# Hybrid attention and MLP block: every second output weight's low part on VectorE, the first weights in two transfers, two forced orders

## The chip, the cores and the metric

The kernel runs on one core of one Trainium2 chip. The metric is the device time of one execution in microseconds (us), as the median of several runs. The engines are named as in the profile: PE (TensorE), DVE (VectorE), ACT (ScalarE), POOL (GpSimd) and SP (SyncE, which issues the transfers of this kernel).

## The reference

One layer of a streaming encoder over x of 1 x 1024 x 1024, float32. Two groups of eight heads of 64 share one input projection: group A is sliding-window attention with two key/value heads and learned sinks, group B is attention over the own chunk of 64 and eight chunks before it, with a relative bias.

```python
n = rms_norm(h, norm1_g[layer])
proj = jnp.einsum('bsd,dp->bsp', n, w_in[layer])
qa, ka, va, qb, kb, vb = jnp.split(proj, split_at, axis=-1)
ya = mixer_a(...)            # sliding window, sinks
yb = mixer_b(...)            # softmax over a band of 9 chunks of 64 keys
y = jnp.concatenate([rms_norm(ya, out_norm_a_g[layer]),
                     rms_norm(yb, out_norm_b_g[layer])], axis=-1)
h = h + jnp.einsum('bsm,md->bsd', y, w_out[layer])
n2 = rms_norm(h, norm2_g[layer])
u = jnp.square(jax.nn.relu(jnp.einsum('bsd,df->bsf', n2, w_ff1[layer])))
h = h + jnp.einsum('bsf,fd->bsd', u, w_ff2[layer])
return rms_norm(h, final_norm_g)
```

## The kernel before

Every operand of a large product is kept as two parts: a high part, a rounded copy that ACT mostly writes, and a low part, the full value minus the high one. The low part is `split_l` (L170), a subtraction of two tiles on whichever engine its caller names; three products of parts stand for one product. So each operand costs one ACT copy and one subtraction on DVE or POOL, and PE's matmuls wait for both.

The program goes through the block in stages: the input projections (`ip_...`) and group A's attention, the transposes and projections of group B, group B's attention (`S_B` scores, `P_B` probabilities, `pt_B` transposes in PSUM, `T_B` their two parts, `av_B` the product with the values) with the output projection (`op_A`, `op_B`) between its pieces, and the MLP (`f`, `f_a`, `f_b`, `f_c`). PE's order is written out by hand and forced (`pe_order`); the other engines take their instructions in an order that a scheduler sets from the dependencies, and `after` (the dictionary is called `turned`) adds single forced orders: one instruction may not stand ahead of a marked one on its engine.

Head pairs of group B are numbered 0 to 7. `self.row` norms one row of probabilities by `rc_B` (L735, TENSOR_SCALAR, 128x640). `split_transposed` (L539) writes the high part of a transposed block T by ACT and the low one by DVE; `padL` is the last, half-empty block. PE's next `pt_B` and `av_B` wait for these.

The output weights w_out come in eight blocks `o0` to `o7` of 128 x 1024 (`out_weight`, L836). `load_weight` moves one block into a stage slot `st_o`, scales it by a gain in ACT for m = 2 and 3 (L221), writes the high part `w0_o` by ACT in two pieces of 128x512 (L222), and the low part `w1_o` by POOL in four pieces of 128x256. A stage slot is free again when the low part of the block in it is done, and a later block's transfer waits for that in SP's queue. o0 to o3 are made around 291 to 306 us, while PE works at the value projection `ip_vB` and group B's attention; o4 to o7 around 364 to 396 us, before `op_B`. Other work of POOL there is `h<-h,o` (L923), which adds the output `o` of `op_A` (L922, ACT) to the residual, and `sqB` (L624), sums of squares for the norm of group B.

At the start, SP moves the first block of x transposed and the first gains (`first`, L299), then the first weights (`first_w`, L300, 256 KB: k in its left half, q in its right), then `second` and others. DVE writes the high part `w_kA`, ACT that of q, and PE's first matmul `ip_kA` waits for them after some matmuls on zeros (`idle_ps`).

In the MLP, `operand` (L1054) splits the combined sums X of the activations, `combined` (L1082) and `sum_of` (L1111) make these sums; `prepare1` makes those for the weights ahead.

```python
return load_weight(w_out[m * P : (m + 1) * P, :], [P, D], f"o{m}", pool, 1, 2,
                   ogc[:, m : m + 1] if m in PLAIN else None)
```

Of the kernel before, what the change touches and what calls it, by code (L numbers as in the profile page):

```python
# [16 lines left out]
P = 128  # L17
SEQ = 1024
D = 1024
# [32 lines left out]
def kernel(  # L52
# [97 lines left out]

            return issue

    turned = {}

    def after(ins, mark=None, key=None):

        if mark:
            turned[mark] = ins.ins.name
        elif key in turned:
            dep = mybir.DependencyInfo(mybir.DependencyClass.NoSync, mybir.DependencyReason.DATA)  # L160
            tc.add_manual_dep(ins.ins, turned.pop(key), dep, reason="program order")

    def matmul(*args, **kw):
        pe(nc.tensor.matmul(*args, **kw))  # L164
# [4 lines left out]
    def split_l(engine, lo, full, hi):  # L169
        return engine.tensor_tensor(lo, full, f(hi), ALU.subtract)  # L170
# [102 lines left out]
    def load_start():  # L273

        ws = {kind: [page([P, NK, P], f"w{hl}_{name}") for hl in range(2)] for kind, _, name, _ in first_three}

        act, dve = InOrder(nc.scalar), InOrder(nc.vector)

        def split_w(kind, p, src, high, wait=False):
            hi, lo = (w[:, 2 * p : 2 * p + 2] for w in ws[kind])  # L280
            src = src.rearrange("p (a b) -> p a b", a=2)
            if high is dve:
                high.tensor_copy(hi, src)
            else:
                high.activation(hi, src, AF.Copy)

            def low():
                split_l(dve, lo, src, hi)

            return low if wait else low()  # L290

        def block(name):
            t = sp.tile([P, 2, HALF], F32, tag="xs", bufs=7, name=name)
            return t.rearrange("p a b -> p (a b)")


        b0, b1 = (block(f"x{k}") for k in range(2))
        w0 = sp.tile([P, D], F32, tag="xr", bufs=4, name="w0")
        nc.sync.dma_start(b0[:, : HALF + 8], first)  # L299
        nc.sync.dma_start(w0[:, :HALF], first_w)  # L300
        nc.sync.dma_start(b1[:, :HALF], second)
        nc.sync.dma_start(b1[:, HALF : HALF + 2 * P].rearrange("p (a b) -> p a b", a=2), w_in[VA0 // P][:, :2])
        dve.tensor_copy(g1c, b0[:, HALF : HALF + 8])
        low = split_w("k", 0, w0[:, : 2 * P], dve, True)
        split_xT(0, 0, b0[:, :HALF], b0[:, HALF : HALF + 1], act, dve)
        low()
        split_w("q", 0, w0[:, 2 * P : HALF], act)
        split_xT(0, 1, b1[:, :HALF], g1c[:, 1:2], act, dve)
        split_w("v", 0, b1[:, HALF : HALF + 2 * P], act)
        for k in range(2, NK):  # L310
            t = block(f"x{k}")
            n = HALF + 2 * P * len(WITH[k])
            nc.sync.dma_start(t[:, :n], start[k - 2][:, :n])
            split_xT(0, k, t[:, :HALF], g1c[:, k : k + 1], act, dve)
            for i, kind in enumerate(WITH[k]):
                c = HALF + 2 * P * i
                split_w(kind, k // 2, t[:, c : c + 2 * P], act)
        return [ws[kind] for kind in "kqv"]
# [217 lines left out]
        return [small.tile([P, 4], F32, tag=t, name=f"{t}_{name}") for t in ("nm", "sm", "rc")]  # L536

    def split_transposed(tp, T, lo, hi):
        after(nc.scalar.activation(T[:, 0, lo:hi], tp, AF.Copy), None, "ACT")  # L539
        low = split_l(nc.vector, T[:, 1, lo:hi], tp, T[:, 0, lo:hi])  # L540
        after(low, None, "DVE")
        turned["low"] = low.ins.name

    sq, late = {}, []

# [165 lines left out]
    class UnitB:  # L711
# [25 lines left out]
        def step(self, n):  # L737
            if n < len(self.kbs):
                self.turn(self.kbs[n])
            if n == 2 and late:  # L740
                turned["row"] = turned["low"]
                late.pop()()
            if n > 1:
                self.apply(self.kbs[n - 2])
# [88 lines left out]

    def out_weight(m):

        return load_weight(w_out[m * P : (m + 1) * P, :], [P, D], f"o{m}", pool, 1, 2, ogc[:, m : m + 1] if m in PLAIN else None)  # L836

    hres = {}

# [60 lines left out]
    def out_proj_a():  # L900
        ys, ws = [], []
        for m in range(4):
            ws.append(out_weight(m))
        for m in range(4):
            ys.append(load_y(m, (0,)))
        yield
        for tb in range(TB):
            if tb == 1:
                for m in range(4):
                    ys[m] += load_y(m, (1,))  # L910
            h = hres[tb] = page([P, D], f"h{tb}", F32)
            nc.sync.dma_start(h, x[tb * P : (tb + 1) * P, :])
            for dh in range(2):
                c = slice(dh * HALF, (dh + 1) * HALF)
                ps = aps.tile([P, HALF], F32, tag="w", bufs=3, name=f"op_A_{tb}_{dh}")
                for q in range(4):
                    out_proj_step(ps, ys, ws, q, tb, c)
                    if q == 3 and (tb, dh) == (TB - 1, 1):
                        yield
                    if q == 3:  # L920
                        o = main.tile([P, HALF], F32, tag="tst", bufs=2, name=f"o{tb}_{dh}")
                        nc.scalar.activation(o, ps, AF.Copy, scale=rA[:, tb : tb + 1])  # L922
                        nc.gpsimd.tensor_tensor(h[:, c], h[:, c], o, ALU.add)  # L923
                    if q < 3 or (tb, dh) != (TB - 1, 1):
                        yield
# [123 lines left out]
    def operand(p, n, g, src, engine):  # L1049

        if p not in X:
            X[p] = [[page([P, 2, HALF], f"X{p}{hl}{i}") for i in range(2)] for hl in range(2)]
        hi, lo = (X[p][hl][g][:, :, part(n)] for hl in range(2))
        nc.scalar.activation(hi, src, AF.Copy)  # L1054
        split_l(engine, lo, src, hi)

    def first_half(d, n, g):

# [49 lines left out]

    def sum_of(a, b, op, name, engine, alloc):
        t = alloc(name)  # L1110
        engine.tensor_tensor(t, a, b, op)  # L1111
        return t

    def second_operands(src, made, p, name, engine, alloc):
# [169 lines left out]
    for at, (n, p) in enumerate(order1):  # L1284
        if p == 3 and n > 0:
            load1(n + 1)
        ahead1 = at + (AHEAD1 + 1 if at < AT_ONCE else AHEAD1)

        behind = (n, p) == (0, 2)
        if ahead1 < len(order1) and not behind:  # L1290
            prepare1(*order1[ahead1], ahead1)
        product1(n, p)
        for work in chores.get((n, p), ()):
            combined(*work)
            if behind and work[0] == 5:
                prepare1(*order1[ahead1], ahead1)
        if n == NQ - 1:
            if p == 6:
                for i in range(LOAD2):
                    fetch2(i)  # L1300
            if p in (3, 7, 2):
                prepare2({3: 0, 7: 1, 2: 2}[p])
# [183 lines left out]
def _lay_out(inputs):  # L1486
    import numpy as np

    a = {n: np.ascontiguousarray(v) for n, v in inputs.items()}
    rel = a["rel_bias_b"][0]  # L1490
    far = np.repeat(rel[:, 256:], 512, axis=1)
    ext = np.concatenate([far, rel[:, 255:0:-1]], axis=1)
    band = np.stack([ext[:, 127 - p : 127 - p + 640] for p in range(128)], axis=1)
    d = -np.abs(128 + np.arange(128)[:, None] - np.arange(256)[None, :]).astype(np.float32)
    d[:64, 192:] = NEG
    d[64:, :64] = NEG
    og = np.concatenate([a["out_norm_a_g"][0], a["out_norm_b_g"][0]]).reshape(8, 128).T
    xT = a["x"][0].T.reshape(8, 128, 2, 512).transpose(2, 0, 1, 3)
    w_in = a["w_in"][0].reshape(8, 128, -1, 128).transpose(2, 1, 0, 3)
    cols = {"k": w_in[KA0 // P], "q": w_in[QA0 // P], "v": w_in[VA0 // P]}  # L1500

    def two(kind, p):
        return cols[kind][:, 2 * p : 2 * p + 2].reshape(128, 256)

    start = np.zeros((6, 128, 1024), np.float32)
    for k in range(2, 8):
        parts = [xT[0, k]] + [two(kind, k // 2) for kind in WITH[k]]
        start[k - 2, :, : 512 + 256 * len(WITH[k])] = np.concatenate(parts, axis=1)
    first = np.concatenate([xT[0, 0], a["norm1_g"][0].reshape(8, 128).T], axis=1)
    first_w = np.concatenate([two("k", 0), two("q", 0)], axis=1)  # L1510
    lay = {
        "x": a["x"][0], "xT": xT[1], "first": first, "first_w": first_w, "second": xT[0, 1], "start": start, "w_in": w_in, "sinks_a": a["sinks_a"][0],
        "relb": band, "dist": d, "og": og, "w_out": a["w_out"][0], "norm2_g": a["norm2_g"][0],
        "w_ff1": a["w_ff1"][0], "w_ff2": a["w_ff2"][0], "final_norm_g": a["final_norm_g"],
    }
    return {n: np.ascontiguousarray(lay[n]) for n in _INS}
# [20 lines left out]
```

## Time and profile before

| | before |
|---|---|
| median of 3 runs | 1057.28 us (1055.93 to 1059.97) |
| the profiled execution's own time | 1059.39 us |
| its span, first to last instruction | 1057.60 us |
| PE busy | 1046.9 us, 99% of the span |
| DVE, ACT, POOL busy | 692.9, 598.5, 434.5 us |
| granted TensorE clock, mean | 0.998 |

The span is what the trace shows; 1.79 us of the profiled time lie around it. A busy PE means only that some matmul is in its pipeline: a matmul of 512 columns takes 0.39 us from start to end, while in an unbroken series one starts every 0.23 us. So a gap between starts can be longer than usual without a wait in the list of waits.

### The profile page before, as it was taken

The numbers are of one execution on the slowest core, as the hardware profiler recorded it, in microseconds if no ns is written. First come the engines' busy times: TensorE is split into PE (matmuls) and PEld (weight loads), VectorE is DVE, ScalarE is ACT, GpSimd is POOL, SyncE is SP. The second block draws the span as 40 slices with busy tenths as digits, with TensorE's granted clock in tenths as the row PEclk, the third lists the DMA queues.
The fourth block names the chain that finished last, engine by engine and source line by source line (L and its number), as shares of the span: only waits on it lengthen the run. The fifth ranks groups of instructions, "written<-read, shape, count | busy, mean of one in ns | idle before, by whom it ended". The sixth has DMA issues, their size and how long they took to land.

```text
span 1057.6 us, 14451 instructions
## 1 busy us (share of the span) xinstructions
PE 1046.9 (99%) x5059; PEld 876.6 (83%) x5059; DVE 692.9 (66%) x1120; ACT 598.5 (57%) x1040; POOL 434.5 (41%) x338
## 2 busy tenths in 40 slices
PE   9999999999989999999999999999999999999997
PEld 7888888888878888888888888888888888888886
DVE  6578675767674645796434425436879877778667
ACT  8677876656676766675554454455533333333347
POOL 0567785323353563205554345344124024024025
PEclk9999999999999999999999999999999999999999
DMA  9944545343484442315535525426997545532004
GB/s 359 258 136 137 143 132 154 103 122 99 129 282 159 140 161 99 120 58 182 183 123 165 185 100 179 159 81 243 369 403 256 179 122 167 178 114 96 1 1 160
DMA packets 73929, 170.18 MB, mean 161 GB/s; under 512 B 7552, under 2 KB 24960, under 8 KB 73856
## 3 DMA queue, kind: packets, MB, share of 16 engines
q1 hardware_dynamic: 73712, 168.99, 48.2%
q8 instruction: 40, 0.66, 0.3%
q14 instruction: 33, 0.27, 0.1%
q10 hardware_dynamic: 144, 0.26, 0.1%
HBM read 105.26 MB, written 45.09 MB: 142 GB/s over the span
## 4 chain that ended last, share of the span: by engine, by line
PE 96%; DVE 2%; ACT 1%; issue 0%; DMA 0%; POOL 0%; ACTq 0%; DVEq 0%
PE f L164 27%; PE f_a L164 16%; PE f_c L164 8%; PE ip_qA L164 4%; PE ip_kB L164 4%; PE ip_qB L164 4%; PE op_B L164 4%; PE f_b L164 4%; PE op_A L164 4%; PE ip_vB L164 4%; PE av_B L164 3%; PE S_B L164 3%; PE pt_B L167 2%; PE S_A L164 1%; PE av_A L164 1%; PE pt_A L167 1%
## 5 line engine op out<-in xcount | busy, mean ns | idle before, releaser
L164 PE MATMUL f<-X,W 128*128 128x512 f32 x1344 | 306.0, 390 | 0.2
L164 PEld LDWEIGHTS f<-X,W 128*128 128x128 f32 x1344 | 252.0, 188 | 53.0 <-DVE X L170 0.6
L170 POOL TENSOR_TENSOR U<-u,U 128x1024 fp32r<-128x1024 f32 x32 | 80.6, 2520 | 226.7 <-PE f_c L164 141.4
L164 PE MATMUL f_a<-V,U 128*128 128x512 f32 x756 | 173.5, 390 | 0.0
L164 PEld LDWEIGHTS f_a<-V,U 128*128 128x128 f32 x756 | 141.9, 188 | 29.6 <-DVE C L1426 0.3
L170 POOL TENSOR_TENSOR W<-T,W 128x1024 fp32r<-128x1024 f32 x29 | 75.6, 2609 | 140.5 <-ACT W L1133 140.5
L164 PE MATMUL f_c<-V,U 128*128 128x512 f32 x384 | 88.4, 390 | 0.0
L1133 ACT ACTIVATE V<-Z 128x1024 fp32r<-128x1024 f32 x32 | 33.9, 1060 | 89.7 <-PE f_a L164 44.6
L164 PEld LDWEIGHTS f_c<-V,U 128*128 128x128 f32 x384 | 72.1, 188 | 15.0
L1133 ACT ACTIVATE V<-w 128x1024 fp32r<-128x1024 f32 x24 | 25.4, 1060 | 81.6 <-issue 34.3
L1182 DVE TENSOR_TENSOR k<-f,k 128x1024 f32<-128x1024 f32 x24 | 29.3, 1221 | 61.9 <-PE f L164 61.9
L170 POOL TENSOR_TENSOR W<-w,W 128x1024 fp32r<-128x1024 f32 x23 | 56.2, 2445 | 32.2 <-ACT W L1133 32.1
L170 DVE TENSOR_TENSOR V<-w,V 128x1024 fp32r<-128x1024 f32 x24 | 49.2, 2055 | 28.3 <-ACT V L1133 28.3
L532 ACT ACTIVATE P_B<-P_B,nm_B 128x640 f32<-128x640 f32 (+2 forms) x64 | 44.4, 695 | 35.0 <-DVE nm_B L529 17.8
L1133 ACT ACTIVATE U<-u 128x1024 fp32r<-128x1024 f32 x56 | 58.5, 1045 | 10.1 <-DMA ud<-k 6.8
L170 DVE TENSOR_TENSOR T_B<-pt_B,T_B 128x512 fp32r<-128x512 f32 (+2 forms) x72 | 39.3, 554 | 28.3 <-ACT T_B L539 27.7
L1176 ACT ACTIVATE k<-f 128x1024 f32<-128x1024 f32 x24 | 24.6, 1026 | 57.8 <-PE f L164 57.8
L1133 ACT ACTIVATE W<-T 128x1024 fp32r<-128x1024 f32 x32 | 33.9, 1059 | 33.4 <-PE f L164 21.0
L170 DVE TENSOR_TENSOR V<-Z,V 128x1024 fp32r<-128x1024 f32 x32 | 45.7, 1427 | 9.0 <-ACT V L1133 6.3
L164 PE MATMUL ip_qA<-nT,w_qA 128*128 128x512 f32 x192 | 50.1, 396 | 0.0
L164 PE MATMUL ip_kB<-nT,w_kB 128*128 128x512 f32 x192 | 49.9, 396 | 0.0
L164 PE MATMUL ip_vB<-nT,w_vB 128*128 128x512 f32 x192 | 49.6, 395 | 0.0
(255 smaller groups left out, 2077.6 us busy)
## 6 DMA issues: line engine op xcount, KB each, us to landing
w<-in_w_ff_dram SPq DMA_DIRECT2D x64, 512.0 KB, 4.7
u<-ud SPq DMA_DIRECT2D x56, 512.0 KB, 4.7
ud<-k SPq DMA_DIRECT2D x48, 512.0 KB, 3.2
KkB<-ts_kB SPq DMA_DIRECT2D x64, 128.0 KB, 2.3
yd<-y SPq DMA_DIRECT2D x14, 512.0 KB, 2.7
y<-yd SPq DMA_DIRECT2D x14, 512.0 KB, 6.4
xr<-in_x_dram SPq DMA_DIRECT2D x8, 512.0 KB, 8.5
QqB<-ts_qB SPq DMA_DIRECT2D x32, 128.0 KB, 2.3
```

What stands on the lines that cost most here:

```text
L164: pe(nc.tensor.matmul(*args, **kw))
L167: pe(nc.tensor.transpose(*args))
L170: return engine.tensor_tensor(lo, full, f(hi), ALU.subtract)
L532: nc.scalar.activation(pr[:, :n], pr[:, :n], AF.Exp, bias=nm, scale=-1.0, accum_out=sm)
L1133: nc.scalar.activation(w[0], full, AF.Copy)
L1176: nc.scalar.activation(kept[p], ps, AF.Copy)
L1182: dve.tensor_tensor(v, ps, v, ALU.add)
```

## The change

Four things are changed. (1) `first_w` is moved as two transfers of 128 KB, k and then q, instead of one. (2) The low parts of o1, o3, o5 and o7 are made by DVE, in two pieces of 128x512, instead of by POOL in four of 128x256. (3) The last `o` of `op_A` (ACT) may not stand ahead of the last high part written by `split_transposed`. (4) One sum of the MLP (`sum_of`, DVE) may not stand ahead of the low part of the operand X made just before. The renaming of `turned` to `marks` changes nothing by itself.

```diff
-        nc.sync.dma_start(w0[:, :HALF], first_w)
+        for n in range(2):
+            c = slice(2 * P * n, 2 * P * (n + 1))
+            nc.sync.dma_start(w0[:, c], first_w[n])
...
     def split_transposed(tp, T, lo, hi):
-        after(nc.scalar.activation(T[:, 0, lo:hi], tp, AF.Copy), None, "ACT")
+        high = nc.scalar.activation(T[:, 0, lo:hi], tp, AF.Copy)
+        after(high, None, "ACT")
+        marks["high"] = high.ins.name
...
     def out_weight(m):
 
-        return load_weight(w_out[m * P : (m + 1) * P, :], [P, D], f"o{m}", pool, 1, 2, ogc[:, m : m + 1] if m in PLAIN else None)
+        return load_weight(w_out[m * P : (m + 1) * P, :], [P, D], f"o{m}", nc.vector if m % 2 else pool, 1, 2, ogc[:, m : m + 1] if m in PLAIN else None)
...
                         yield
+                        marks["exit"] = marks["high"]
                     if q == 3:
                         o = main.tile([P, HALF], F32, tag="tst", bufs=2, name=f"o{tb}_{dh}")
-                        nc.scalar.activation(o, ps, AF.Copy, scale=rA[:, tb : tb + 1])
+                        after(nc.scalar.activation(o, ps, AF.Copy, scale=rA[:, tb : tb + 1]), None, "exit")
...
-        split_l(engine, lo, src, hi)
+        marks["operand"] = split_l(engine, lo, src, hi).ins.name
...
-        engine.tensor_tensor(t, a, b, op)
+        after(engine.tensor_tensor(t, a, b, op), None, "sum")
...
             if behind and work[0] == 5:
+                marks["sum"] = marks["operand"]
                 prepare1(*order1[ahead1], ahead1)
...
-    first_w = np.concatenate([two("k", 0), two("q", 0)], axis=1)
+    first_w = np.stack([two("k", 0), two("q", 0)])
```

PE's order is the same in both kernels. On DVE the eight new pieces stand at five places. The first is ahead of the transposed blocks of head pair 5, at about 293 us of the trace before (ISA is the scores' bias and maximum, L529; numbers of tiles are kept). Before:

```order
L529 ISA P_B4_1_0_3752,nm_B4_1_3748<-S_B4_1_0_3751,b_B4_3388 128x640
L529 ISA nm_B4_1_3748 128x1
L529 ISA P_B4_1_1_3762,nm_B4_1_3748<-S_B4_1_1_3761,b_B4_3388 128x640
L529 ISA nm_B4_1_3748 128x1
L170 TENSOR_TENSOR T_B5_0_0_3738<-pt_B5_0_0_3733,T_B5_0_0_3738 128x512
L170 TENSOR_TENSOR T_B5_0_1_3745<-pt_B5_0_1_3741,T_B5_0_1_3745 128x384
L351 TENSOR_TENSOR ts_vB3_0_3785<-ip_vB3_0_3712,R1_163 128x512
L734 RECIPROCAL rc_B4_1_3750<-sm_B4_1_3749 128x1
L735 TENSOR_SCALAR P_B4_1_0_3752<-P_B4_1_0_3752,rc_B4_1_3750 128x640
```

And in the changed kernel:

```order
L170 TENSOR_TENSOR w1_o1_3673<-st_o1_3671,w0_o1_3672 128x512
L531 ISA P_B4_1_0_3749,nm_B4_1_3745<-S_B4_1_0_3748,b_B4_3389 128x640
L531 ISA nm_B4_1_3745 128x1
L170 TENSOR_TENSOR w1_o1_3673<-st_o1_3671,w0_o1_3672 128x512
L531 ISA P_B4_1_1_3759,nm_B4_1_3745<-S_B4_1_1_3758,b_B4_3389 128x640
L531 ISA nm_B4_1_3745 128x1
L170 TENSOR_TENSOR T_B5_0_0_3735<-pt_B5_0_0_3730,T_B5_0_0_3735 128x512
L170 TENSOR_TENSOR T_B5_0_1_3742<-pt_B5_0_1_3738,T_B5_0_1_3742 128x384
L353 TENSOR_TENSOR ts_vB3_0_3782<-ip_vB3_0_3709,R1_163 128x512
L738 RECIPROCAL rc_B4_1_3747<-sm_B4_1_3746 128x1
L739 TENSOR_SCALAR P_B4_1_0_3749<-P_B4_1_0_3749,rc_B4_1_3747 128x640
```

Both pieces of o1 now stand ahead of the two T_B of pair 5; the two pieces of o3 come some rows further down. The second place is on DVE too, among the transposed blocks of head pair 6, at about 369 us. Before:

```order
L170 TENSOR_TENSOR T_B6_1_2_4514<-pt_B6_1_2_4510,T_B6_1_2_4514 128x384
L529 ISA P_B7_1_1_4531,nm_B7_1_4482<-S_B7_1_1_4530,b_B7_4066 128x640
L529 ISA nm_B7_1_4482 128x1
L170 TENSOR_TENSOR T_B6_1_3_4525<-pt_B6_1_3_4520,T_B6_1_3_4525 128x512
L734 RECIPROCAL rc_B7_1_4484<-sm_B7_1_4483 128x1
L735 TENSOR_SCALAR P_B7_1_1_4531<-P_B7_1_1_4531,rc_B7_1_4484 128x640
L170 TENSOR_TENSOR T_B6_1_4_4551<-pt_B6_1_4_4546,T_B6_1_4_4551 128x512
```

And in the changed kernel:

```order
L170 TENSOR_TENSOR T_B6_1_2_4511<-pt_B6_1_2_4507,T_B6_1_2_4511 128x384
L531 ISA P_B7_1_1_4528,nm_B7_1_4479<-S_B7_1_1_4527,b_B7_4063 128x640
L531 ISA nm_B7_1_4479 128x1
L170 TENSOR_TENSOR w1_o5_4655<-st_o5_4653,w0_o5_4654 128x512 x2
L170 TENSOR_TENSOR T_B6_1_3_4522<-pt_B6_1_3_4517,T_B6_1_3_4522 128x512
L738 RECIPROCAL rc_B7_1_4481<-sm_B7_1_4480 128x1
L739 TENSOR_SCALAR P_B7_1_1_4528<-P_B7_1_1_4528,rc_B7_1_4481 128x640
```

Both pieces of o5 stand directly ahead of the low part of T_B6_1_3. The third place is SP's queue behind the transfers of o3 and o4; y0 is the normed group A output that `op_A` reads. Before:

```order
L120 DMA st_o3_3692<-in_w_out_dram 128x1024
L120 DMA st_o4_4642<-in_w_out_dram 128x1024
L831 DMA y0_0_3704<-yd_86 128x1024
L831 DMA y0_1_3706<-yd_86 128x1024
L831 DMA y0_2_3708<-yd_86 128x1024
L831 DMA y0_3_3710<-yd_86 128x1024
L567 DMA b_B6_4062<-in_relb_dram 128x640
L120 DMA st_o5_4656<-in_w_out_dram 128x1024
```

And in the changed kernel:

```order
L120 DMA st_o3_3691<-in_w_out_dram 128x1024
L120 DMA st_o4_4639<-in_w_out_dram 128x1024
L120 DMA st_o5_4653<-in_w_out_dram 128x1024
L835 DMA y0_0_3701<-yd_86 128x1024
L835 DMA y0_1_3703<-yd_86 128x1024
L835 DMA y0_2_3705<-yd_86 128x1024
L835 DMA y0_3_3707<-yd_86 128x1024
L571 DMA b_B6_4059<-in_relb_dram 128x640
```

The transfer of o5 has moved ahead of the four loads of y0.

## Rows read from the trace of the kernel before

**Rows 1.** The page: busy us of each engine, share, instructions.

```profile
PE 1046.9 (99%) x5059; PEld 876.6 (83%) x5059; DVE 692.9 (66%) x1120; ACT 598.5 (57%) x1040; POOL 434.5 (41%) x338
```

**Rows 2.** The waits of PE in the whole span.

```profile
PE vt_vB L167 <- DVE T_B L170: 3.0, 1, 3.0
PE idle_ps L164 <- DVE eps L106: 0.9, 1, 0.9
PE ip_kA L164 <- ACT w_qA L145: 0.4, 1, 0.4
```

**Rows 3.** The chain that ended last, 290 to 312 us.

```profile
298.06 4.59 DVE P_B L735
...
302.75 0.55 DVE P_B L735
```

**Rows 4.** Timeline of ACT, POOL, DVE and PE, 290 to 306 us.

```profile
291.66 2.18 ACT L222 ACTIVATE w_o<-st_o 128x512 fp32r<-128x512 f32 x4
...
292.48 9.82 POOL L170 TENSOR_TENSOR w_o<-st_o,w_o 128x256 fp32r<-128x256 f32 x14
...
293.87 0.82 DVE L529 CUSTOM_DVE_ANT_0 P_B<-S_B,b_B 128x640 f32<-128x640 f32 x1 [2.51 <-PE S_B L164]
...
295.37 1.15 DVE L170 TENSOR_TENSOR T_B<-pt_B,T_B 128x512 fp32r<-128x512 f32 x2
...
297.01 0.38 PE L167 MATMUL pt_B<-ident,P_B 128*128 128x128 f32 x2
```

**Rows 5.** Groups by form, DVE (busy us, mean ns of one).

```profile
L790 DVE TENSOR_TENSOR Y<-Y,yc 128x512 f32<-128x512 f32 x1 | 0.7, 694 | 1.7 <-ACT yc L787 1.7
```

**Rows 6.** Timeline of DVE and POOL, 441 to 447 us.

```profile
443.81 2.48 DVE L170 TENSOR_TENSOR X<-S,X 128x512 fp32r<-128x512 f32 x1 [0.18 <-ACT X L1054]
...
443.34 2.40 POOL L170 TENSOR_TENSOR W<-w,W 128x1024 fp32r<-128x1024 f32 x1 [13.96 <-ACT W L1133]
```

**Rows 7.** Timeline of POOL, DVE and PE, 364 to 374 us.

```profile
368.04 1.30 POOL L624 TENSOR_TENSOR sqB<-sqB,y 128x512 f32<-128x512 f32 x1
369.30 1.28 POOL L923 TENSOR_TENSOR h<-h,o 128x512 f32<-128x512 f32 x1
370.54 3.80 POOL L170 TENSOR_TENSOR w_o<-st_o,w_o 128x256 fp32r<-128x256 f32 x5
...
369.24 0.69 DVE L170 TENSOR_TENSOR T_B<-pt_B,T_B 128x512 fp32r<-128x512 f32 x1
...
370.34 0.49 PE L167 MATMUL pt_B<-ident,P_B 128*128 128x128 f32 x3
```

**Rows 8.** Timeline of SP and PE, 288 to 316 us (SPq: an issue).

```profile
298.58 2.11 SPq L831 DMA_DIRECT2D y<-yd  x4
...
312.01 2.33 PE L164 MATMUL op_A<-w_o,y 128*128 128x512 f32 x9
```

**Rows 9.** DMA issues of 298 to 312 us (KB each, median us to landing).

```profile
y<-yd SPq DMA_DIRECT2D x5, 512.0 KB, 6.5
```

**Rows 10.** Timeline of ACT and PE, 386 to 389 us.

```profile
386.34 0.69 ACT L922 ACTIVATE o<-op_A,rgA 128x512 f32<-128x512 f32 x1 [1.42 <-PE op_A L164]
386.92 0.37 ACT L539 ACTIVATE T_B<-pt_B 128x256 fp32r<-128x256 f32 x1
...
387.35 0.84 PE L164 MATMUL av_B<-T_B,VvB 128*128 128x256 f32 x2
...
388.03 0.40 PE L164 MATMUL av_B<-padL,VvB 128*128 128x256 f32 x2
```

**Rows 11.** Timeline of PE, 459.1 to 459.6 us.

```profile
458.77 1.02 PE L164 MATMUL f<-X,W 128*128 128x512 f32 x2
```

**Rows 12.** Timeline of DVE and PE, 0 to 12 us.

```profile
4.30 0.30 DVE L145 CAST w_kA<-w 128x256 fp32r<-128x256 f32 x1 [0.48 <-DMA w<-in_first_w_dram]
...
9.62 0.75 DVE L145 SCALAR_TENSOR_TENSOR nT<-x,g1c,nT 128x512 fp32r<-128x512 f32 x1 [0.32 <-ACT nT L145]
...
4.75 0.77 PE L164 MATMUL ip_kA<-nT,w_kA 128*128 128x512 f32 x1 [0.44 <-ACT w_qA L145]
```

More of the change, by code (lines that the diff above doesn't have):

```diff
@@ L151, in __getattr__ @@
             return issue
-    turned = {}
+    marks = {}
     def after(ins, mark=None, key=None):
         if mark:
-            turned[mark] = ins.ins.name
-        elif key in turned:
+            marks[mark] = ins.ins.name
+        elif key in marks:
             dep = mybir.DependencyInfo(mybir.DependencyClass.NoSync, mybir.DependencyReason.DATA)
-            tc.add_manual_dep(ins.ins, turned.pop(key), dep, reason="program order")
+            tc.add_manual_dep(ins.ins, marks.pop(key), dep, reason="program order")
     def matmul(*args, **kw):
@@ L538, in split_transposed @@
     def split_transposed(tp, T, lo, hi):
-        after(nc.scalar.activation(T[:, 0, lo:hi], tp, AF.Copy), None, "ACT")
+        high = nc.scalar.activation(T[:, 0, lo:hi], tp, AF.Copy)
+        after(high, None, "ACT")
+        marks["high"] = high.ins.name
         low = split_l(nc.vector, T[:, 1, lo:hi], tp, T[:, 0, lo:hi])
         after(low, None, "DVE")
-        turned["low"] = low.ins.name
+        marks["low"] = low.ins.name
     sq, late = {}, []
@@ L740, in step @@
             if n == 2 and late:
-                turned["row"] = turned["low"]
+                marks["row"] = marks["low"]
                 late.pop()()
```

## The prediction

> **What bounds the kernel now.** I read the page first: PE is busy 1046.9 us, 99% of the span [rows 1], so only what makes PE wait or start late can move the time. The list of PE's waits has three entries, 3.0, 0.9 and 0.4 us [rows 2]; the reader should see that nothing else on the chip is worth even 0.1%. The largest, 3.0 us before `vt_vB`, I followed up the chain of waits: one norm of probabilities on DVE takes 4.59 us from 298.06, and the next of the same form takes 0.55 [rows 3]. The timeline of the same stretch shows why: POOL runs 14 low pieces of output weights back to back from 292.48 to 302.30, 0.70 each, and the long DVE row ends 0.35 after the last of them [rows 4]. So DVE was held for 4.04 us behind six POOL pieces, and the T_B that PE needs stood behind it.
>
> Smaller delays don't show as waits, only as stretched series. At 458.77 a pair of matmuls of 512 columns takes 1.02 us [rows 11]; with starts 0.23 apart and 0.39 for one, as in an unbroken series, it would be 0.62, so 0.4 is lost. At 387.35 a pair of `av_B` of 256 columns takes 0.84, and the same form 0.40 at 388.03 [rows 10]: 0.44 lost. Everything that the four edits can reach is therefore 3.0 + 0.4 (the first matmul) + 0.4 + 0.4, about 4 us or 0.4%. That is below 0.5% (5.3 us), about what a measurement of this kernel can tell from no change.
>
> **Output weights, first place (-3.0, then +1.05).** POOL loses o1's four pieces and o3's, so its stream of 14 shrinks to eight at this place and the norm at 298.06 no longer meets an unbroken row; I take the whole 3.0 off. But the two pieces of o1 now stand on DVE ahead of the T_B of pair 5. One costs what a DVE subtraction of 128x512 with both inputs in SBUF costs undisturbed, 0.69 [rows 5], some 0.63 of it before the next can start. I work the chain by hand. ACT's third high part is done at 291.66 + 3 x 0.545 = 293.3 [rows 4]. A POOL piece is running then until 293.9; I let DVE wait for the end of the piece that is running and no longer. That is what the pair at 443.8 shows: DVE's X takes 2.48 from 443.81, where one alone costs 0.69, and ends 0.55 after POOL's W, which ran from 443.34 to 445.74 [rows 6]. So o1's first piece is done at 294.5, the first ISA (0.75 each, two from 293.87 to 295.37 [rows 4]) at 295.3, o1's second piece waits for one more POOL piece until 295.8 and is done at 296.4, the second ISA at 297.2, the low part of T_B at 297.8. Before, that T_B began at 295.37, and PE's `pt_B` came at 297.01 [rows 4]. PE now waits until 297.85: 0.85, and I add 0.2, an estimate, for o3's two pieces, which stand ahead of the values' low part at 305 to 306. Bounds: 0 if DVE never waits for POOL, 3.7 if each piece waits as long as the norm at 298.06 did (293.3 + 4.04 + 0.65 + two ISAs, o1b and T_B = 300.7). I take the rule of row 443.81, because it is two single instructions against each other, as here.
>
> A rule of the skill bears on this. The Trainium skill, SBUF — State Buffer, section "SBUF: two separate sides", says that DVE and GpSimd share a port pair by an exclusive lock: a DVE instruction with two SBUF inputs and a GpSimd one block each other, and whichever starts first holds it for its whole length. The row at 443.81 agrees (1.93 waited, POOL done at 445.74); the row at 298.06 goes beyond it, since by that rule its wait would have ended with the piece then running, 0.7 at most, and PE's 3.0 would not exist. The rule speaks against moving the subtractions to DVE while POOL keeps the even blocks. By the rule the sum is the one below; by the length of the row at 298.06 it is the last rival.
>
> **Output weights, second place (+2.85).** Here nothing was lost before: T_B ran at 369.24 for 0.69 and PE's `pt_B` followed at 370.34 [rows 7]. Now both pieces of o5 stand directly ahead of that T_B. The first needs a buffer that `sqB` reads until 368.04 + 1.30 = 369.34; by then `h<-h,o` has begun at 369.30 and holds until 370.58 [rows 7]. So o5's first piece ends at 371.2. POOL's next low piece of o4 gets in between, until 371.9; o5's second piece ends at 372.5, T_B at 373.1, and PE starts at about 373.2 instead of 370.34: 2.85. Queued behind on DVE are a reciprocal, the T_B after it and the norm of pair 7, all for the same PE row, which has moved by as much, so they cost nothing more. Bounds: 2.15 if DVE's second piece follows its first without POOL between, 0.95 if `h<-h,o` does not hold DVE (369.35 + 2 x 0.63 + T_B = 371.2), 0 if DVE is not held at all and o5's buffer is free earlier than I read it, 4.95 if the first piece waits 4.04 as the norm did. I take 2.85, by the same row as above.
>
> **Third and fourth place, and SP (0).** o3's pieces fall at about 303 to 305.4, when POOL's stream has ended, and o7's at about 392.5 to 393.8, while PE is in the series of `op_B` that follows the last `av_B` at 388.03 [rows 10] and comes to o7 last. Work of PE that doesn't read them covers both; if it were gone, each place costs its two pieces, 1.4. In SP's queue the transfer of o5 now stands ahead of the four loads of y0 and waits for o2's stage slot, free at about 300.1 after POOL's last o2 piece. The loads, issued from 298.58 before [rows 8], are issued from 300.6 to 302.2. A load lands 6.5 us after issue [rows 9]: 307.1 to 308.7. The first `op_A` came at 312.01 [rows 8], which without the 3.0 and with 0.85 back is 309.9. The margin is 2.8 for the first, and the fourth is read nine matmuls of 0.23 later, so its margin is larger. I count zero.
>
> **The last o behind T_B (-0.4).** ACT ran `o` for 0.69 from 386.34 and T_B's high part only at 386.92 [rows 10]. With T_B first, it starts when its transpose is there, some 0.5 earlier; PE's gap of 0.44 closes, but for a few hundredths. `o` then ends at about 387.6, and `op_B`, which waits for its PSUM buffer, comes only after the `av_B` of 388.03 [rows 10]: hidden. Bounds 0 and -0.45.
>
> **The sum behind X (-0.3).** The sum that stood in front of the operand goes behind it; PE's gap of 0.4 closes in its larger part [rows 11]. The moved sum is late by one X, 0.6, and used some 4 us later: hidden. Bounds 0 and -0.4.
>
> **First weights in two (0).** PE's first matmul starts at 4.75, after DVE's `w_kA` of 4.30 to 4.60, which waited for the transfer [rows 12]. Half the bytes may land about 0.3 earlier. But PE is caught again shortly after, by the low part of nT that DVE makes from 9.62 to 10.37 for a matmul at 10.4 [rows 12]; that chain begins with another transfer, so what is won at 4.75 is waited for there. The extra issue pushes the later transfers back by one issue of about 0.45, so the bounds are -0.3 and +0.45. I take the middle, 0.
>
> **The sum.** Against the profiled execution's own 1059.39: -3.0 + 1.05 + 2.85 - 0.4 - 0.3 + 0 = +0.2, so 1059.6. The median before, 1057.28, stands 2.1 below that execution, perhaps because the hold at 298.06 is not as long in every run; from the median the same sum gives 1057.5. I forecast the middle, 1058.5: the wait moves from 304 to 297 and 373, and nothing measurable is won.
>
> **The rivals.**
> Second place cheap: `h<-h,o` doesn't hold DVE, 0.95 instead of 2.85. For it: no row shows this form of POOL's holding DVE, and T_B itself ran beside it in 0.69 [rows 7]. Against: T_B reads PSUM, and row 443.81. 1056.6, chance 0.20.
> DVE hardly waits anywhere: neither new stall, -3.7 - 0.2 in all, 1054.5 (1053.4 from the median, 1055.5 from the profiled run). For it: the ISA and both T_B from 293.87 on ran at their usual length beside POOL [rows 4]. Against: they read PSUM, and the hold on 298.06 is in the trace. 0.12, a sixth of it past 0.5%.
> One of the two places is held through several POOL pieces as at 298.06, 1060 to 1061: 0.13.
> The other side: both are held for 4.04, first place 3.7 and second 4.95, together 8.65 in place of 3.9: 1063.3, slower by 0.55%. It decides from 4.1 us more than forecast, so only if both reach nearly the length of the row at 298.06. For it: POOL still runs two streams of four pieces there; against: these streams are shorter, 2.8 us each. 0.06.
> The forecast has the rest, 0.49, with a range of its own of 1057.3 to 1059.7.
>
> **The numbers.** The range 1054.5 to 1061 holds the forecast, the cheap second place, the single hold and most of the third case; outside lie the double hold and half of the third case, with their tails, under 0.2. Faster by over 0.5% (below 1052.0) 0.04, slower (above 1062.6) 0.06, within 0.90.
>
> **What would show it.** Right: the wait of `vt_vB` is gone from PE's list; new waits on T_B stand at about 297 (0.9) and 370 (2.9); w_o pieces on DVE last clearly over 0.69 at both; no P_B row of several us; `av_B` at 387 and f at 456 in even steps; first matmul earlier, but the matmul at 10 us not. Wrong: no wait at 370, or a DVE w_o row of 3 us or more, or `op_A` waiting for y.

## The result and the profile after

The changed kernel takes 1060.75 us (median of 22 runs, 1059.7 to 1062.17), the kernel before 1056.73 (22 runs, 1055.93 to 1061.74): a ratio of 1.0034, 95% interval [1.0027, 1.0042]. That is 4.0 us slower, clear of noise and still inside the 0.5% that the forecast called no change; the forecast was 1058.5 with a range up to 1061. The profiled execution of the change took 1061.59, its span 1059.8.

The waits of PE in the whole span (us in total, times, longest), to be held against [rows 2]:

```profile
PE pt_B L167 <- DVE rc_B L738: 2.5, 1, 2.5
PE ip_kA L164 <- ACT nT L145: 1.2, 2, 0.9
PE idle_ps L164 <- DVE eps L106: 0.9, 1, 0.9
PE pt_B L167 <- DVE T_B L170: 0.6, 1, 0.6
PE ip_kA L164 <- DVE nT L145: 0.3, 1, 0.3
```

The 3.0 before `vt_vB` is gone, and the two forecast waits on T_B stand there, 0.6 and 2.5 (for the second the list names `rc_B`, DVE's next instruction behind that T_B, which ends 0.07 after it). New is a wait of up to 0.9 at the start, on nT. The timeline of POOL, DVE and PE at the first place of the output weights answers to [rows 4]:

```profile
293.59 3.28 POOL L170 TENSOR_TENSOR w_o<-st_o,w_o 128x256 fp32r<-128x256 f32 x4
...
294.46 1.11 DVE L170 TENSOR_TENSOR w_o<-st_o,w_o 128x512 fp32r<-128x512 f32 x1 [1.99 <-ACT w_o L222]
...
296.23 1.18 DVE L170 TENSOR_TENSOR w_o<-st_o,w_o 128x512 fp32r<-128x512 f32 x1
...
298.08 1.15 DVE L170 TENSOR_TENSOR T_B<-pt_B,T_B 128x512 fp32r<-128x512 f32 x2
...
298.91 0.41 PE L167 MATMUL pt_B<-ident,P_B 128*128 128x128 f32 x2 [0.64 <-DVE T_B L170]
```

Each DVE piece takes 1.11 or 1.18 where one alone takes 0.69 [rows 5]: it waits for one POOL piece and no more. PE's `pt_B` comes 1.90 after its place in the trace before, and 1.1 of that is the start, below. So the stall is 0.8. The second place, POOL, DVE and PE, answers to [rows 7]:

```profile
366.68 1.30 POOL L628 TENSOR_TENSOR sqB<-sqB,y 128x512 f32<-128x512 f32 x1
367.94 1.28 POOL L928 TENSOR_TENSOR h<-h,o 128x512 f32<-128x512 f32 x1
369.19 2.30 POOL L170 TENSOR_TENSOR w_o<-st_o,w_o 128x256 fp32r<-128x256 f32 x2
...
368.01 2.90 DVE L170 TENSOR_TENSOR w_o<-st_o,w_o 128x512 fp32r<-128x512 f32 x2 [0.18 <-POOL sqB L628]
370.83 0.68 DVE L170 TENSOR_TENSOR T_B<-pt_B,T_B 128x512 fp32r<-128x512 f32 x1
...
371.65 0.52 PE L167 MATMUL pt_B<-ident,P_B 128*128 128x128 f32 x3 [2.53 <-DVE rc_B L738]
371.93 0.78 PE L164 MATMUL av_B<-T_B,VvB 128*128 128x512 f32 x2
372.50 1.27 PE L164 MATMUL S_B<-KkB,QqB 128*128 128x320 f32 x4
373.57 3.30 PE L164 MATMUL op_A<-w_o,y 128*128 128x512 f32 x9
```

DVE's two pieces begin 0.03 after `sqB` has ended, wait for `h<-h,o` and then for one piece of o4, and take 2.90 together; T_B follows, PE stands for 2.5. Then something comes that the forecast has not: the nine matmuls of `op_A` take 3.30, where 2.1 to 2.3 is usual (2.33 at its first place, [rows 8]). The windows of PE show it (us, PE busy, number of instructions, granted clock, DMA share, GB/s):

```profile
364.00:368.00 4.00, 3.96 (x25) 1.00 0.02 4
368.00:372.00 4.00, 1.47 (x12) 1.00 0.03 11
372.00:376.00 4.00, 4.00 (x14) 0.57 0.75 253
376.00:380.00 4.00, 4.00 (x23) 1.00 0.12 34
```

```profile
373.00:375.00 2.00, 2.00 (x7) 0.50 0.88 299
```

After 2.5 us without work the granted clock falls: its mean over the four us behind the wait is 0.57, and from 373 to 375 it is 0.50, its lower level of 1.2 GHz. `op_A`'s matmuls start 0.43 apart there, where 0.23 is usual. Between `pt_B` and the end of that stretch PE falls back by another 1.5.

The start, as ACT, PE and SP show it (SPq: an issue), and the landing time of the second block of x (KB, us from issue to landing):

```profile
6.56 0.72 ACT L145 ACTIVATE nT<-x,g1c 128x512 fp32r<-128x512 f32 x1 [1.79 <-DMA x<-in_second_dram]
...
7.33 0.49 PE L164 MATMUL ip_kA<-nT,w_kA 128*128 128x512 f32 x1 [0.94 <-ACT nT L145]
...
2.11 0.43 SPq L303 DMA_DIRECT2D x<-in_second_dram  x1
```

```profile
x<-in_second_dram SPq DMA_DIRECT2D x1, 256.0 KB, 4.4
```

PE's first matmul starts at 4.41 instead of 4.75 [rows 12], but the second block of x is issued at 2.11 and lands at about 6.5, and PE runs dry before it. From 8 us on PE is 1.1 behind. The last two edits, the order of ACT and PE around `op_B` and the series of `f`:

```profile
390.19 0.68 ACT L927 ACTIVATE o<-op_A,rgA 128x512 f32<-128x512 f32 x1
```

```profile
390.56 0.49 PE L164 MATMUL av_B<-padL,VvB 128*128 128x256 f32 x2
390.92 1.42 PE L164 MATMUL op_B<-w_o,y 128*128 128x512 f32 x5
```

```profile
461.31 1.07 PE L164 MATMUL f<-X,W 128*128 128x512 f32 x4
```

The four `f` take 3 x 0.23 + 0.39 = 1.08 for an unbroken series, and 1.07 stand there: the gap of [rows 11] has closed. `av_B` has no gap any more, but `o` now ends at 390.87 and `op_B` starts right behind, 0.05 later; five of it take 1.42 where 1.31 is usual. Some 0.2 is given back.

The distance between the starts of the same matmuls in the two traces adds up to this, in us: start +1.1; first place +0.8 and the hold of [rows 3] -3.1; second place +2.7; granted clock +1.5; `o` behind T_B -0.3 and +0.2; sum behind X -0.3; the remaining -0.4 in steps of at most 0.2, half of it between 304 and 314 us. Together 2.2, the difference of the two spans.

### The profile page after: what moved, and what is told of

Same layout as the page of the kernel before. It is cut to its first block, busy times and chain, and to the rows that moved or that the text cites. A ratio compares the mean times of both kernels' runs of the same rounds, so it can differ in the third digit from the quotient of the medians.

```text
span 1059.8 us, 14446 instructions
## 1 busy us (share of the span) xinstructions
PE 1048.2 (99%) x5059; PEld 877.1 (83%) x5059; DVE 699.8 (66%) x1128; ACT 598.6 (56%) x1040; POOL 423.5 (40%) x322
## 4 chain that ended last, share of the span: by engine, by line
PE 98%; DVE 1%; DMA 0%; POOL 0%; issue 0%; ACT 0%; SPq 0%; ACTq 0%
PE f L164 29%; PE f_a L164 16%; PE f_c L164 8%; PE ip_kB L164 4%; PE op_B L164 4%; PE ip_qB L164 4%; PE ip_vB L164 4%; PE f_b L164 4%; PE ip_qA L164 4%; PE op_A L164 4%; PE av_B L164 3%; PE S_B L164 3%; PE pt_B L167 2%; PE S_A L164 1%; PE av_A L164 1%; PE pt_A L167 1%
```

## The experiments

All ratios are to the kernel before, measured beside it on the same chip.

**The first weights in two transfers, alone.** The kernel before with

```diff
-        nc.sync.dma_start(w0[:, :HALF], first_w)
+        for n in range(2):
+            c = slice(2 * P * n, 2 * P * (n + 1))
+            nc.sync.dma_start(w0[:, c], first_w[n])
```

and `first_w` stacked as in the change.

> The first weights in two transfers, alone. Theory 1 (the shift between the two traces is a sum of places): the start costs what it cost in the changed kernel, 1.06 us from the ninth or so matmul on, and nothing gives it back, so 1.0 us above the kernel before, and no wait on T_B or w_o that before has not. Rival (all the loss is the DVE pieces; the start is caught up behind the first projections): 0.0, within 0.2.

1057.61 against 1056.96, ratio 1.0006 [0.9995, 1.0016]: 0.65 above by the medians, not clear of noise. The profile shows the mechanism clearly, though: PE waits 0.6, 0.5 and 0.3 at the start, on nT, on the q half and on nT again, and is 1.3 behind the first trace of the kernel before at 8.4 us. Behind that the distance changes only at 304, where the wait of 3.0 isn't there, though POOL's stream has its 14 pieces as before. Chance moves the start too: the matmul that comes at 81.95 in the first trace stands between 81.7 and 82.8 in the nine profiles with one transfer of 2 KB rows, at 83.4 here and at 83.1 in the change, later than in any of them.

**The change without the two transfers.** One transfer again, everything else as changed (the first hunk of the diff and its last undone).

> The change without its two transfers (one transfer of 256 KB as before; DVE pieces and both forced orders stay). Theory 1: PE waits about 0.8 at 297 to 299 and 2.5 to 2.9 at 370, forced orders give 0.3 back, so 2.9 us above the kernel before, more by 1.5 in an execution in which the granted clock falls after the longer wait. Rival (the start costs nothing): 4.0 above, as the whole change.

1060.05, ratio 1.0026 [1.0017, 1.0036], 3.1 above: near the 2.9 of theory 1, under the 4.0 of the rival. Six of its 12 runs took 1058.9 to 1059.6, with a mean granted clock of 0.999 or 1.0; five with 0.997 or 0.998 took 1060.5 to 1061.4 (the twelfth, 1060.6, shows 0.999). Between the two groups lie 1.0 to 2.5 us, where the trace has 1.6 for the fallen clock.

**The two forced orders alone.** The second half of the change, `pool` back in `out_weight`, one transfer.

> The two forced orders alone. Theory 1: 0.3 to 0.4 us below the kernel before, almost all from the moved sum at 459; the gap at 387 closes but op_B then waits for the output o by about 0.2. In the profile the list of PE's waits is as in the kernel before, with or without the 3.0 at 304. Rival (a forced order only moves the gap): 0.0.

1055.87, ratio 0.9991 [0.998, 1.0003]. The medians differ by 1.1, the traces only by 0.45 between 384 and 460 us; the interval holds both and zero too. The profile has no wait at 304 either.

**o3, o5, o7 on DVE, o5 behind the T_B.** One transfer, both forced orders, o1 on POOL again, and o5's pieces forced behind the last block:

```diff
-        return load_weight(..., nc.vector if m % 2 else pool, ...)
+        return load_weight(..., nc.vector if m in (3, 5, 7) else pool, ...)
...
-                        split_l(low_engine, w[1][:, c], st[:, c], w[0][:, c])
+                        low = split_l(low_engine, w[1][:, c], st[:, c], w[0][:, c])
+                        if name == "o5":
+                            marks["turn5"] = marks["low"]
+                            after(low, None, "turn5")
```

> DVE makes the low parts of o3, o5 and o7 (o1 is POOL's again), o5's two pieces are forced behind the last T_B block of head pair 6, one first transfer, both forced orders. Theory 1 (the loss is where DVE pieces stand ahead of a T_B that PE is about to take): no wait at 297 or 370, no fall of the clock, 0.3 us below the kernel before. Rival (it is the port: any DVE piece with two SBUF inputs beside a POOL stream costs, wherever it stands): a new wait of 1 us or more somewhere between 300 and 380, above the kernel before.

1056.6 against 1056.96, ratio 0.9992 [0.9983, 1.0], as theory 1 has it. PE's list has only the start left, and the six DVE pieces show as no more than a `pt_B` at 377 that comes 0.3 late. The rival isn't tested by this, though, because none of the six stands beside a POOL stream: o3's pieces come behind the end of POOL's stream, and o5's two fall into a pause of POOL (rows of POOL and DVE in order of time).

```profile
292.36 8.94 POOL L170 TENSOR_TENSOR w_o<-st_o,w_o 128x256 fp32r<-128x256 f32 x12
...
301.95 0.68 DVE L170 TENSOR_TENSOR w_o<-st_o,w_o 128x512 fp32r<-128x512 f32 x1
...
372.19 1.28 DVE L170 TENSOR_TENSOR w_o<-st_o,w_o 128x512 fp32r<-128x512 f32 x2
...
374.59 1.29 POOL L929 TENSOR_TENSOR h<-h,o 128x512 f32<-128x512 f32 x1 [3.20 <-ACT o L928]
```

So the new places are free of both, of a T_B that PE is about to take and of POOL. What a piece beside POOL costs behind such a T_B was not run.

**The kernel before, profiled again.** No edit.

> The kernel before, profiled once more. Theory 1 (the hold of a DVE norm over six POOL pieces at 298 is a chance event of the execution first shown): here the norm takes 1.1 us, PE has no wait before vt_vB, and the time is 1056 to 1057. Rival (the hold belongs to the program): the wait of about 3 us stands there again and the time is 1059.

1056.16 in its one run, and no wait at 304. The timeline of DVE and POOL at the place of [rows 3] and [rows 4]:

```profile
298.13 1.11 DVE L735 TENSOR_SCALAR P_B<-P_B,rc_B 128x640 f32<-128x640 f32 x1
...
299.34 0.84 DVE L735 TENSOR_SCALAR P_B<-P_B,rc_B 128x640 f32<-128x640 f32 x1
...
292.55 10.33 POOL L170 TENSOR_TENSOR w_o<-st_o,w_o 128x256 fp32r<-128x256 f32 x14
```

The same POOL stream of 14, the same program, and the norm takes 1.11 instead of 4.59: it got in behind one piece, and POOL's stream is longer for it, 10.33 instead of 9.82. The hold of the first trace was a chance event of that execution. The times agree: 19 of the 22 executions of the kernel before took 1055.93 to 1058.17, the other three 1059.69 to 1061.74; whether the hold is in those isn't recorded.

**o5 alone on DVE.** `nc.vector if m == 5 else pool`, one transfer, both forced orders.

> Of the output weights only o5's low part is DVE's, in its two pieces ahead of T_B of pair 6; o1, o3 and o7 are POOL's; one first transfer, both forced orders. Theory 1 (the loss is this place): PE waits about 2.5 at 371 and the granted clock falls afterwards in some executions, so 2.7 us above the two forced orders alone, 1.6 to 2.6 above the kernel before. Rival (o1 and the port at 297 are the larger part): within 0.5 of the kernel before.

1061.08 (5 runs, 1059.44 to 1061.6), ratio 1.0039 [1.0026, 1.0051]: 4.5 above by the medians, more than either theory. The wait at 371 is there, 2.5. But this profile, of a run of 1061.6, also has a wait of 0.4 on a transfer (`S_A`, at about 52 us), and the hold again, in the waits of PE, on DVE and on POOL:

```profile
PE vt_vB L167 <- DVE T_B L170: 1.9, 1, 1.9
```

```profile
298.96 3.19 DVE L737 TENSOR_SCALAR P_B<-P_B,rc_B 128x640 f32<-128x640 f32 x1
...
293.38 8.42 POOL L170 TENSOR_TENSOR w_o<-st_o,w_o 128x256 fp32r<-128x256 f32 x12
```

and its granted clock behind the wait at 371 stayed at 1.00, `op_A` at its usual length:

```profile
374.23 2.23 PE L164 MATMUL op_A<-w_o,y 128*128 128x512 f32 x9
```

The DMA engines were at least as busy there as in the change:

```profile
374.00:376.00 2.00, 2.00 (x11) 1.00 0.99 366
```

So busy DMA engines don't make the long `op_A` of the change; the clock does. The fall of the clock and the hold don't need each other: the change has the first without the second, this profile the second without the first. The lowest run, 1059.44, is 2.9 above the median before, 0.3 more than the upper end of theory 1; what the other three runs had isn't shown beyond a mean clock of 0.997 or 0.998 in each of them.

**One transfer of 1 KB rows.** The kernel before, the stacked `first_w` in one transfer.

```diff
-        nc.sync.dma_start(w0[:, :HALF], first_w)
+        nc.sync.dma_start(w0[:, :HALF].rearrange("p (a b) -> p a b", a=2), first_w.rearrange("a p b -> p a b"))
```

> The kernel before, its first weights in one transfer as before, but from the stacked layout, so that each partition gets two rows of 1 KB instead of one of 2 KB. Theory 1a (the start loses because every later transfer is issued 0.47 later): no loss, 0.0. Theory 1b (it loses because smaller rows take longer and hold up the transfers behind them): the second block of x lands at about 6 us as with two transfers, 0.6 above the kernel before.

1057.07 against 1056.58, ratio 1.0006 [0.9997, 1.0015]: 0.5 above by the medians, not clear of noise. The landing of the second block of x tells more:

```profile
6.29 0.72 ACT L145 ACTIVATE nT<-x,g1c 128x512 fp32r<-128x512 f32 x1 [1.42 <-DMA x<-in_second_dram]
```

It is issued at 1.65 as before, and lands 4.6 us later; in the two profiles of the kernel before it took 3.3 and 3.8, and in the nine profiles with one transfer of 2 KB rows 3.3 to 4.3. So 4.6 has the sign of theory 1b, but lies only 0.3 above the highest of the others: rows half as long may delay what is behind them without a further issue; one profile doesn't show it. Nor does PE wait for the block here. Its matmuls start 0.43 apart until about 10.6 us, as at the lower clock above (the trace has no record of the clock so early), and so it comes to the block only when that has landed:

```profile
7.60 1.48 PE L164 MATMUL ip_kA<-nT,w_kA 128*128 128x512 f32 x3
```

In the trace before the same three take 0.84. So this profile can't tell what the later landing costs.

**One residual add left out.** The change with one transfer; POOL doesn't add `op_A`'s output for rows 640 to 767, columns 512 to 1023.

```diff
-                        nc.gpsimd.tensor_tensor(h[:, c], h[:, c], o, ALU.add)
+                        if (tb, dh) != (5, 1):
+                            nc.gpsimd.tensor_tensor(h[:, c], h[:, c], o, ALU.add)
```

> The change with one first transfer, and one residual add left out: POOL doesn't add the output of op_A for rows 640 to 767, columns 512 to 1023, so this part of the result lacks group A's share. That add is what POOL runs when DVE comes to o5. Theory 1 (DVE waits for the end of the POOL instruction that is running): DVE's first o5 piece then waits for a low piece of o4 of 0.7 instead of the add of 1.28, PE's wait at 371 falls by 0.5 to 0.6, from 2.5 to 1.9 or 2.0. Rival (the two DVE pieces are late for another reason, such as the buffer that sqB reads): the wait stays at 2.5.

1059.59 in its one run; the wait falls from 2.5 to 2.0. DVE and POOL at the place:

```profile
366.68 2.34 DVE L170 TENSOR_TENSOR w_o<-st_o,w_o 128x512 fp32r<-128x512 f32 x2 [0.18 <-POOL sqB L626]
...
366.61 1.86 POOL L170 TENSOR_TENSOR w_o<-st_o,w_o 128x256 fp32r<-128x256 f32 x2
```

The pair takes 2.34 instead of 2.90, less by 0.56; POOL's running instruction is shorter by 1.28 - 0.70 = 0.58. DVE waits for the end of what POOL is running. A pair that meets no POOL instruction takes 1.28, so about 1.6 of the 2.90 in the change are waits on POOL.

**All four on DVE, o5 behind the T_B.** As the fourth experiment, with `nc.vector if m % 2 else pool`.

> The change with one first transfer and o5's two DVE pieces forced behind the last T_B of head pair 6; o1, o3 and o7 stay where they are on DVE. Theory 1 (the price of o5 is where it stands): no wait at 371, no fall of the clock behind it; 0.6 to 0.8 at 297 remains, the forced orders give 0.3, so 0.3 to 0.6 above the kernel before, and about 3 below the same kernel without this order. Rival (two pieces beside POOL cost the same anywhere in this stretch): 3 above.

1057.09 against 1056.65, ratio 1.0001 [0.9992, 1.001]: 0.4 above the kernel before, where the same kernel with o5 ahead was 3.1 above, so 2.7 below it. PE's list has 0.6 on T_B at 297 and nothing at 371. o5 on DVE, now that POOL's stream is over:

```profile
372.84 1.28 DVE L170 TENSOR_TENSOR w_o<-st_o,w_o 128x512 fp32r<-128x512 f32 x2
```

Two pieces in 1.28, where 2.90 were taken ahead of T_B. The forced order moves them out of POOL's way and behind T_B at once; it doesn't tell the two apart. Behind them a `pt_B` at 378 comes 0.3 late.

**o1 alone on DVE.** `nc.vector if m == 1 else pool`, one transfer, both forced orders.

> Of the output weights only o1's low part is DVE's, ahead of the T_B of pair 5; both forced orders, one first transfer. Theory 1: PE waits 0.8 at 297 and nothing at 371; POOL still makes o2 and o3 in a row, so the norm behind can be held for more than a piece, by chance; 0.5 above the kernel before. Rival (o1's place is free of cost, the rest is o5's): 0.3 below.

1057.29, ratio 1.0004 [0.9995, 1.0013], 0.6 above by the medians as expected, not clear of noise; PE waits 0.6 on T_B, its `pt_B` comes 0.8 late, and there is no wait at 371.

**Two transfers, the second block of x between them.**

```diff
-        nc.sync.dma_start(w0[:, :HALF], first_w)
+        nc.sync.dma_start(w0[:, : 2 * P], first_w[0])
         nc.sync.dma_start(b1[:, :HALF], second)
+        nc.sync.dma_start(w0[:, 2 * P : HALF], first_w[1])
```

> The kernel before with the first weights in two transfers, and the second block of x issued between them, at the place in the queue that it has in the kernel before. Theory 1 (the start loses since the second block of x comes later): it lands up to half a us earlier than with both halves ahead of it, and the loss of 0.6 goes to 0.2 or less, though the q half is now later for PE's second matmul. Rival (two transfers of 1 KB rows cost the same in any order): 0.6 above the kernel before.

1059.07, ratio 1.0018 [1.0008, 1.0029], 2.4 above: both theories missed the time. The second block does land earlier, 4.0 after its issue at 1.65, but PE's second matmul, on the q half, starts only at 7.52:

```profile
7.05 0.42 ACT L145 ACTIVATE w_qA<-w 128x256 fp32r<-128x256 f32 x1 [2.66 <-DMA w<-in_first_w_dram]
```

```profile
7.52 0.65 PE L164 MATMUL ip_qA<-nT,w_qA 128*128 128x512 f32 x1 [2.58 <-ACT w_qA L145]
```

The q half, issued fourth at 2.12, is used 4.9 later, though it has only 128 KB. In all three kernels with two transfers the fourth of the queue is first used at 6.5 to 7.1 us: the second block of x in the change (6.56) and alone (6.83), here the q half (7.05). PE needs both, the q half sooner, and so this order is the dearer one. A second loss follows in this profile: behind PE's wait of 2.6 the granted clock is at its lower level,

```profile
8.00:10.00 2.00, 2.00 (x6) 0.50 1.03 418
```

and PE, 2.6 behind the second profile of the kernel before at that matmul, is 3.3 behind it at 11 us. How many of the other runs had this fall isn't shown.

## Why the prediction was right, and where not

That nothing is won was right, and 1060.75 lies inside the range of 1054.5 to 1061, but only 0.25 under its upper end and outside the forecast's own 1057.3 to 1059.7. The sum said +0.2 against the kernel before; measured is +4.0. That the range still held it is in part luck: its upper end was there for a single hold through several POOL pieces, which the trace of the change doesn't have. Half a per cent was too coarse a bound as well, since the measurement, with an interval of 0.15%, tells 0.34% from nothing.

Of the two starting points of the sum, the profiled execution with the hold in it gave 1059.6, where start and clock are missing; the median gave 1057.5 by taking off a hold that the median doesn't have.

**Output weights, first place, -3.0.** This is the step that failed. The step took a hold of 4.04 us in one profiled execution for a property of the program and took the whole 3.0 off. The kernel before without a change shows 1.11 for the same norm, of the six profiles with this POOL stream of 14 pieces only that first one has the hold, and a program with another stream of POOL has it. In most executions of the kernel before there was nothing to win here. The text noticed that the median stood 2.1 under the profiled execution and even named the reason as a possibility, and then took the middle. Counted from the median, with nothing taken off, the rest of the forecast would have given 1057.28 + 1.05 + 2.85 - 0.7 = 1060.5.

**First place, +1.05.** Measured 0.8 between the traces and 0.6 by o1 alone; the chain by hand (o1b done at 296.4, T_B 297.8) runs 1.1 us ahead of the trace throughout, by the start, and is otherwise right within 0.2. The extra 0.2 for o3 didn't come.

**Second place, +2.85.** Measured 2.7 between the traces; DVE's pair, POOL's add and the one piece of o4 between stand as written. Leaving out the add shows that DVE waits for POOL's running instruction; with o5 behind the T_B, where POOL pauses too, PE's wait is gone. By the lengths of the pair, 2.90 and 1.28, some 1.6 of the 2.7 are waits on POOL and the rest the pieces themselves. That the order alone would take it away, with POOL still running, is argued and not shown. The Trainium skill, SBUF — State Buffer, section "SBUF: two separate sides", says that whichever of the two engines starts first has the shared port pair for its whole instruction and the other is blocked until then. The waits agree: 1.11, 1.18 and 2.90 are the ends of the running POOL instructions plus the pieces' own length. The holds of 4.59 and 3.19 go beyond it: by that rule neither could pass the end of the piece then running, 0.7 us, as far as the rule covers the norm, which reads one tensor and a 128x1 scalar.

**What the forecast had not: the clock.** No step asked what PE's standing still for 2.5 us does to what follows. In the profile of the change, in that without the two transfers, and in that without the add, the mean granted clock is 0.57 to 0.59 over the four us behind the wait, with 0.50 in its middle, which costs 1.5 to 1.6 us in each; with o5 alone it stayed at 1.00 after the same wait. In the trace of before the wait of 3.0 wasn't followed by a fall either. So it is an event of some executions. Of the 22 of the change it was perhaps in seven: they have mean clocks of 0.997 or 0.998 and took 1061.5 to 1062.2, while the others, at 0.999 or 1.0, took 1059.7 to 1061.1; the means of the two groups differ by 1.4. The mean clock alone doesn't tell, since the first profile of the kernel before has 0.998 without such a fall. What decides it was not found.

**First weights, 0.** Mis-sized: 0.65 by the medians alone, 1.1 between the traces, outside the given bounds of -0.3 and +0.45 in the trace. The step priced the additional issue, 0.45, and took the landing time of the second block of x as given. It lands 4.4 after an issue that is 0.46 later, instead of 3.3; alone the two transfers have 4.6, the one transfer with 1 KB rows 4.6 at the old issue, and the nine profiles with 2 KB rows 3.3 to 4.3. So the later issue is shown, and the slower landing is likely. The second block was what PE needs next, at about 6.3 us, ahead of the low part at 10 us on which the step rested.

**The last o, -0.4.** Half wrong: the gap closed, but `o` is not hidden; `op_B` needs its PSUM buffer at about the time when `o` ends. Net -0.1. **The sum behind X, -0.3**: as forecast. **Third and fourth place and SP, 0**: as forecast; `op_A` waits for no y.

So the measured 4.0 is, with start and first place as the experiments have them alone and the rest from the traces: start 0.65, first place 0.6 to 0.8, second place 2.7, orders -0.35 to -0.45, and the clock 1.5 in perhaps a third of the runs, 0.5 in the mean. That adds up to 4.0 to 4.3. No version that was run is faster than the kernel before beyond its interval; the two forced orders alone (0.9991) and o3, o5, o7 with o5 late (0.9992) come nearest.

## What to carry to other kernels

Look at a stall in a single profiled execution with the spread of the times beside it: if that execution is slower than the median by about the stall, the stall is perhaps not in the median, and a second profile of the same kernel settles it for little. Work moved from a busy helper engine to another costs where it stands: ask which instruction that the critical engine is about to need stands behind it, and what runs beside it on the engine that it was taken from. And a wait of a few us on the engine with a granted clock can cost more than itself.

## What the runs showed of the hardware

A DVE norm of 128x640, 0.55 alone and 1.1 where it began just ahead of a POOL piece, took 4.59 us in one execution and 3.19 in another, while POOL ran six and four pieces past it. In both the norm began 0.022 to 0.023 us ahead of the next POOL piece by the records of the trace; in the six profiles where it began so and was not held (the kernel before again, the forced orders alone, the two transfers alone, the 1 KB rows, the second block between, o5 late without o1) 0.005 to 0.017 ahead. Eight cases show that a few ns may decide; that they do isn't shown.

The granted clock fell to 0.50, the lower level, behind waits of 2.0 to 2.6 us of PE in four profiles (the change, without the two transfers, without the add, the second block between), and not behind waits of 2.5 and 3.0 in two others.

The transfer behind one early 256 KB transfer landed 3.3 to 4.3 us after its issue in nine profiles with rows of 2 KB, and 4.6 in one with rows of 1 KB; a chance difference isn't excluded.
